# One level of Strassen's algorithm in an up-projection, and a down-projection that reads its features from DRAM

## The chip, the cores and the metric

The program runs on one core of a Trainium2 chip. The core has five engines that work side by side and meet through semaphores: TensorE (PE: matrix products into PSUM, with its weight loads shown apart as PEld), VectorE (DVE), ScalarE (ACT), GpSimd (POOL) and SyncE (SP, which here only issues DMAs). The metric is the device time of one execution in microseconds (us); a kernel's time is the median of its runs. A span is the time from the first to the last instruction of one profiled execution.

## The reference

One residual block of a streaming encoder: 1024 frames of width 1024, with 16 meta tokens in front (1040 tokens), all in float32. An input projection feeds two attention branches of 8 heads each; their outputs are projected, gated, added, and projected once more by `w_out`. Then comes the part that the change touches:

```python
h  = h + rms_norm(mixed, gains[1])                 # mixed = (gated sum) @ w_out
xn = rms_norm(h, gains[2])                         # 1040 x 1024
u  = causal_depthwise_conv(xn @ w_up, conv_w, conv_b)   # w_up 1024 x 5632, 3 taps over time
u_gate, u_val = split(u, 2)                        # 2816 each
ffn = (gelu(u_gate) * u_val) @ w_down              # w_down 2816 x 1024
h  = h + rms_norm(ffn, gains[3])
return h[:, 16:]                                   # the meta tokens are dropped
```

## The kernel before

**Layout.** Features lie on the 128 partitions, tokens along the free axis. A width of 1024 is 8 tiles of 128 (`KT`), the feed-forward width of 2816 is 22 (`NK`). From line 526 on only the last 1026 tokens are kept (`NA`: 1024 frames and the two before them, which the three taps of the convolution need), in three pieces of 342 (`PCA`).

**Products in three terms.** TensorE runs in its reduced-precision float32 mode (`F32R`). To keep the precision, each operand is split into a rounded part and a remainder (`hi`, `lo`), and `products` (line 111) adds `hi*hi + hi*lo + lo*hi`: three matmuls where one would be. A weight tile comes in through `load_w` (line 95): one DMA into `wraw` (three buffers), a cast on ACT into `whi`, a subtraction on GpSimd or VectorE into `wlo` (two buffers each).

**Stages.** Lines 61 to 523 do the attention. Lines 526 to 574 project and gate the branches. `merge(i, o)` (587) multiplies by `w_out`, piece by piece, 24 matmuls of 342 columns each; `norms(i)` (604) takes the first RMS norm of a piece, adds the residual, writes it to DRAM (`hd`), splits the sum, scaled by the second norm's gains, into `x2h` and `x2l`, and makes the second norm's factor `rs2`, by which the up-projection's result is multiplied as it leaves PSUM (line 654). So the up-projection's matmuls need the split sum, not the finished second norm. While the last piece is normalized (`tail`, lines 660 to 672), TensorE already has the first two pieces' up-projection of two weight tiles to do, ordered by hand with `after` (`tc.issue_after`).

**The feed-forward part.** `up_tile(k)` (681) makes the gate tile and the value tile of 128 features each: 3 pieces x 8 input tiles x 3 terms = 72 matmuls of 342 columns for each, then the three taps (ACT line 694, VectorE line 696 twice), the gelu (699), the product (701) and the split into `gh`, `gl`, which stay in SBUF. Groups of 4, 4, 4, 4 and 6 such tiles (`GROUPS`) are multiplied by `w_down`: `down` (714) accumulates one group in PSUM and adds it to `acc` (722, 724), one group behind the up-projection, in columns of 512. The last group goes by `last_down` (750) in columns of 256 so that the last norm (`last_norm`, 765) and the output follow each quarter.

**What sets the order.** Each engine has a queue that it works off in order. The order in it is made when the program is built: among the instructions whose inputs are due by a planner's own costs, the one that stands first in the program text goes first. Tiles of one tag share their buffers, and a pool that is opened where an earlier one was closed takes over its memory, tile by tile, each new tile waiting for the tiles that lay there (`reuse_waits="tile"`). All DMAs of this part are issued by SP, in one queue, except half of the output's, which ACT issues.

## Time and profile before

| | |
|---|---|
| median of 3 runs | 1752.41 us (1752.24 to 1753.49) |
| the profiled execution's own time | 1753.54 us |
| its span | 1751.5 us |
| mean granted TensorE clock | 0.981 |
| PE busy | 1691.4 us (97%), 10716 matmuls |
| DVE, ACT, POOL busy | 986.5, 704.3, 690.0 us |
| moved by DMA | 127.32 MB, mean 73 GB/s |

Matmuls are pipelined and their ends are modelled, so PE's busy share does not say how close it is to its peak: the rate is read from the starts of matmuls that follow one another, or from a stage's time divided by their number. A stall shows as idle time of an engine with the name of what ended it. In a group's row "x" is the number of instructions, then stand their busy time in us and the mean of one in ns.

### The profile page before, as it was taken

How to read it: one execution, taken by the hardware profiler on the slowest of the kernel's cores; microseconds unless marked ns; L12 is line 12 of the kernel's file. 1: busy time of each engine (PE TensorE's matmuls, PEld its weight loads, DVE VectorE, ACT ScalarE, POOL GpSimd, SP SyncE). 2: the span in 40 equal slices, each digit the busy share in tenths (PEclk: the TensorE clock that was granted, in tenths of full speed). 3: DMA queues.
4: the chain of work that ended last, by engine and by line, in shares of the span. 5: the costliest groups of instructions: out<-in, count | busy, mean ns of one | idle time of the engine just before them, and what ended most of it. 6: DMA issues, size and time to landing. Idle time of an engine off the chain costs nothing.

```text
span 1751.5 us, 27046 instructions
## 1 busy us (share of the span) xinstructions
PE 1691.4 (97%) x10716; PEld 1635.1 (93%) x10716; DVE 986.5 (56%) x1652; ACT 704.3 (40%) x1409; POOL 690.0 (39%) x423
## 2 busy tenths in 40 slices
...
GB/s 165 65 57 74 60 60 62 62 57 52 38 43 41 36 41 64 62 211 145 139 167 161 123 51 25 57 52 31 54 61 31 42 71 27 36 73 49 29 129 109
DMA packets 57166, 127.32 MB, mean 73 GB/s; under 512 B 10160, under 2 KB 31920, under 8 KB 56272
## 3 DMA queue, kind: packets, MB, share of 16 engines
...
## 4 chain that ended last, share of the span: by engine, by line
PE 84%; DVE 8%; issue 3%; ACT 2%; DMA 2%; POOL 1%; SPq 0%; DVEq 0%; ACTq 0%; POOLq 0%
PE pu L116 27%; PE pd L710 14%; PE pq L116 9%; PE pg L116 9%; PE y L116 5%; PE pv L116 4%; PE po L429 4%; PE pm L116 3%; PE tr L419 3%; PE s L347 2%; PE s L346 2%; DVE xl L127 1%; DVE kp L396 1%; PE tm L409 1%; DMA oraw<-od 1%
## 5 line engine op out<-in xcount | busy, mean ns | idle before, releaser
L654 DVE TENSOR_TENSOR u<-pu,rs 128x342 f32<-128x342 f32 x132 | 67.4, 513 | 260.9 <-PE pu L116 256.4
L116 PE MATMUL pu<-x2h,wl_u 128*128 128x342 f32 x1056 | 190.0, 321 | 3.7 <-DVE wl_u L90 3.7
L90 POOL TENSOR_TENSOR wl_u<-wr_u,wh_u 128x1024 fp32r<-128x1024 f32 x40 | 96.1, 2401 | 245.7 <-ACT wh_u L104 166.6
L116 PE MATMUL pu<-x2h,wh_u 128*128 128x342 f32 x1056 | 190.2, 322 | 0.6 <-DVE u L654 0.6
L116 PE MATMUL pu<-x2l,wh_u 128*128 128x342 f32 x1056 | 189.0, 321 | 0.0
L116 PEld LDWEIGHTS pu<-x2h,wl_u 128*128 128x128 f32 x1056 | 172.1, 190 | 4.0 <-DVE wl_u L90 4.0
L116 PEld LDWEIGHTS pu<-x2h,wh_u 128*128 128x128 f32 x1056 | 171.8, 190 | 1.4 <-DVE u L654 0.9
L116 PEld LDWEIGHTS pu<-x2l,wh_u 128*128 128x128 f32 x1056 | 172.1, 190 | 0.0
L696 DVE SCALAR_TENSOR_TENSOR c<-u,cb,c 128x1024 f32<-128x1024 f32 (+1 forms) x100 | 135.4, 1357 | 57.4 <-ACT c L694 55.9
L391 POOL TENSOR_SCALAR pr<-pr,mx 128x144 f32<-128x144 f32 (+3 forms) x64 | 114.9, 1801 | 102.6 <-DVE mx L390 63.6
L399 POOL TENSOR_TENSOR pr<-pr,kp 128x143 f32<-128x143 f32 (+3 forms) x64 | 80.6, 1260 | 120.9 <-DVE kp L396 69.5
L424 DVE TENSOR_TENSOR pt<-tr,pt 128x512 fp32r<-128x512 f32 (+1 forms) x160 | 98.2, 631 | 36.8 <-ACT pt L423 34.3
L429 PE MATMUL po<-pt,vv 128*128 128x256 f32 (+1 forms) x640 | 109.9, 282 | 7.7 <-DVE pt L424 5.9
L104 ACT CAST wh_u<-wr_u 128x1024 fp32r<-128x1024 f32 x44 | 46.2, 1051 | 167.1 <-PE pu L116 125.7
L429 PEld LDWEIGHTS po<-pt,vv 128*128 128x128 f32 x640 | 94.4, 190 | 9.8 <-DVE pt L424 6.9
L710 PE MATMUL pd<-gl,wh_d 128*128 128x512 f32 x256 | 101.1, 395 | 0.0
L710 PE MATMUL pd<-gh,wl_d 128*128 128x512 f32 x256 | 101.1, 395 | 0.0
L710 PE MATMUL pd<-gh,wh_d 128*128 128x512 f32 x256 | 101.1, 395 | 0.0
L423 ACT CAST pt<-tr 128x512 fp32r<-128x512 f32 (+1 forms) x160 | 83.1, 545 | 35.5 <-PE tr L419 33.8
L90 POOL TENSOR_TENSOR wl_d<-wr_d,wh_d 128x512 fp32r<-128x512 f32 x32 | 41.4, 1295 | 141.1 <-ACT wh_d L104 95.2
L419 PE MATMUL tr<-cs,pr 128*128 128x128 f32 x576 | 91.0, 274 | 0.0
L384 ACT ACTIVATE pr<-s,mx 128x144 f32<-128x144 f32 (+6 forms) x112 | 59.8, 541 | 75.9 <-DVE mx L382 60.5
...
## 6 DMA issues: line engine op xcount, KB each, us to landing
...
```

The costliest lines, as they stand in the source:

```text
L90: eng.tensor_tensor(dst, a, f(hi), op=ALU.subtract)
L116: marks["mm"] = nc.tensor.matmul(ps, w[:, k * P : (k + 1) * P], x[:, k - k0, n0:n1], start=(k == k0 and s == 0), stop=(k == k1 - 1 and s = ...
L384: nc.scalar.activation(pr[:, s0:s1], pss[k][:, : s1 - s0], AF.Exp, bias=m, scale=-1.0, accum_out=mx[:, 4 + k : 5 + k])
L391: nc.gpsimd.tensor_scalar(pr[:, :w], pr[:, :w], z, None, op0=ALU.mult)
L399: nc.gpsimd.tensor_tensor(pr[:, : w - 1], pr[:, : w - 1], kp[:, 1:w], op=ALU.mult)
L419: nc.tensor.transpose(tr[:, x * P : (x + 1) * P], prs[tb][:, NM + j * P : NM + (j + 1) * P], ident)
L423: nc.scalar.copy(pt[:, 0, :n], tr[:, :n])
L424: nc.vector.tensor_tensor(pt[:, 1, :n], tr[:, :n], f(pt[:, 0, :n]), op=ALU.subtract)
L429: nc.tensor.matmul(po[:, o0:256], vj, pt[:, s, 256 * j : min(256 * j + 256, n)], start=False, stop=(last and j == 1 and s == 1))
L654: nc.vector.tensor_tensor(u[:, n0:n1], ps, rs2[:, n0:n1], op=ALU.mult)
L696: nc.vector.scalar_tensor_tensor(cc, u[:, c0 + tap : c1 + tap], cb[:, x, tap : tap + 1], cc, op0=ALU.mult, op1=ALU.add)
L710: nc.tensor.matmul(ps, w[:, k * P : (k + 1) * P], x[:, c0:c1], start=(k == 0 and s == 0), stop=(k == len(gs) - 1 and s == 2))
```

## The change

**The up-projection** of a gate tile and its value tile is taken as one 2 x 2 block product. On the left, the weights: rows gate (`a11`, `a12`) and value (`a21`, `a22`), columns the first and second half of the 1024 input features. On the right, the normalized input: rows its two halves of features, columns two halves of tokens of 514 each (`HT`; the two tokens in the middle are in both, for the taps). In Winograd's form of Strassen's algorithm seven block products replace eight, at the price of sums: four on the weights per pair of tiles (`s1` to `s4`), four on the input once (`t1` to `t4`), and sums of the results. Each block product is 4 input tiles x 3 terms x two pieces of 258 and 256 columns (`BL`): 24 matmuls. A pair of tiles has 168 matmuls where it had 144, of 257 columns where it had 342.

**Around it.** The second norm is now applied to the input itself, before it is split (`norms`, its last loop), since the sums need a common scale. The seven right factors are split and kept in SBUF: `b11` and `b21` during the merge of the last piece, the five others after its norms, in two slices of columns (0 to 172, 172 to 514). The products that were ordered by hand under the last norms are gone, and with them `rs2`, `x2h`, `x2l`.

**The down-projection** comes after the whole up-projection. The gated features of each tile go to DRAM (`gdr`). They are read back in three column blocks of 512, 256 and 256 tokens (`DP`), split (`hidden`), and multiplied by all of `w_down` for each block (`down`), accumulating all 22 tiles in PSUM; the loads and the splits of `w_down` are done three times, in chunks of 8, 7 and 7 tiles. The additions to `acc` are gone; ACT takes the squares and the scaled copy straight from PSUM.

The core of the diff (the lines of the branch projections, lines 535 to 574, only change their indentation and the pool they are in; `parts(i)` names the token half or halves, `xh2[0]` and `xh2[1]`, into which a piece falls):

```diff
-GROUPS = [4, 4, 4, 4, 6]
+NB = NX // 2
+HT = NB + 2
+DP = [(0, 512), (512, 768), (768, 1024)]
...
+    px1 = pc.enter_context(ExitStack())
+    xc1 = px1.enter_context(tc.tile_pool(name="xc1", reuse_waits="tile", bufs=1))
+    right = {}
+    def right_tiles(pool, names):
+        for n in names:
+            right[n] = (pool.tile([P, 4, HT], F32R, name=f"rh_{n}"), pool.tile([P, 4, HT], F32R, name=f"rl_{n}"))
+    right_tiles(xc1, ("b11", "b21"))
+    pxh = ExitStack()
+    xhp = pxh.enter_context(tc.tile_pool(name="xhp", reuse_waits="tile", bufs=1))
+    xh2 = [xhp.tile([P, KT, HT], F32, name=f"xn{i}") for i in range(2)]
+    phn = ExitStack()
+    hp = phn.enter_context(tc.tile_pool(name="hp", reuse_waits="tile", bufs=1))
+    psA = pc.enter_context(tc.tile_pool(name="psA", reuse_waits="tile", bufs=4, space=PSUM))
+    psN_ = ExitStack()
+    psN = psN_.enter_context(tc.tile_pool(name="psN", reuse_waits="tile", bufs=2, space=PSUM))
...
+    def norms(i):
...
+        for k in range(KT):
+            for x, c in hs:
+                nc.scalar.activation(mg[:, k, c], x[:, k, :], AF.Copy, scale=gn[:, 2, k : k + 1])
+        rs = rstd_row(sqs, w, hp, psN, "ms", f"c{i}").unsqueeze(1)
+        for x, c in hs:
+            for k in range(0, KT, 4):
+                nc.vector.tensor_tensor(x[:, k : k + 4, :], mg[:, k : k + 4, c],
+                                        rs[:, :, c].to_broadcast([P, 4, c.stop - c.start]), op=ALU.mult)
+    def split(name, x, c, eng):
+        h, l = right[name]
+        nc.scalar.copy(h[:, :, c], x)
+        sub(eng, l[:, :, c], x, h[:, :, c])
+    for i in range(len(PCA)):
+        for o in range(KT):
+            merge(i, o)
+            if i and o == 1:
+                norms(i - 1)
+            if i == 2 and o == 4:
+                nc.gpsimd.tensor_copy(xh2[1][:, :, 0:2], xh2[0][:, :, NB : NB + 2])
+                for k, n in enumerate(("b11", "b21")):
+                    split(n, xh2[0][:, 4 * k : 4 * k + 4, :], slice(0, HT), nc.gpsimd)
+    pm.close()
+    norms(len(PCA) - 1)
+    phn.close()
+    psN_.close()
+    xc2 = pc.enter_context(tc.tile_pool(name="xc2", reuse_waits="tile", bufs=1, side="right"))
+    right_tiles(xc2, ("t2", "b22", "t3", "t4", "t1"))
+    xtp = pxh.enter_context(tc.tile_pool(name="xtp", reuse_waits="tile", bufs=1))
+    for c in (slice(0, 172), slice(172, HT)):
+        w = c.stop - c.start
+        b11, b21 = (xh2[0][:, k : k + 4, c] for k in (0, 4))
+        b12, b22 = (xh2[1][:, k : k + 4, c] for k in (0, 4))
+        t1, t2 = (xtp.tile([P, 4, WMX], F32, tag=t, name=f"{t}_{c.start}")[:, :, :w] for t in ("t1", "t2"))
+        nc.vector.tensor_tensor(t1, b12, b11, op=ALU.subtract)
+        nc.vector.tensor_tensor(t2, b22, t1, op=ALU.subtract)
+        split("t2", t2, c, nc.vector)
+        nc.gpsimd.tensor_tensor(b12, b22, b12, op=ALU.subtract)
+        split("b22", b22, c, nc.vector)
+        split("t3", b12, c, nc.gpsimd)
+        nc.vector.tensor_tensor(b21, b21, t2, op=ALU.subtract)
+        split("t4", b21, c, nc.vector)
+        split("t1", t1, c, nc.gpsimd)
+    pxh.close()
...
+    gdr = [dr.tile([P, NX], F32, name=f"gdr{k}") for k in range(NK)]
+    pu = ExitStack()
+    up = pu.enter_context(tc.tile_pool(name="up", reuse_waits="tile", bufs=2))
+    psR = pu.enter_context(tc.tile_pool(name="psR", reuse_waits="tile", bufs=2, space=PSUM))
+    BL = [(0, 258), (258, HT)]
+    def left_factors(k):
+        raws = []
+        for s in range(2):
+            raw = (wp if s == 0 else up).tile([P, KT * P], F32, tag="wraw" if s == 0 else "vraw",
+                                              bufs=3 if s == 0 else 1, name=f"wu{k}{s}")
+            nc.sync.dma_start(raw, wup[2 * k + s])
+            raws.append(raw)
+        g, v = raws
+        a11, a12, a21, a22 = g[:, 0:512], g[:, 512:1024], v[:, 0:512], v[:, 512:1024]
+        sa_ = up.tile([P, 1024], F32, tag="sA", bufs=1, name=f"sA{k}")
+        sb_ = up.tile([P, 1024], F32, tag="sB", bufs=1, name=f"sB{k}")
+        s2, s4, s3, s1 = sa_[:, 0:512], sa_[:, 512:1024], sb_[:, 0:512], sb_[:, 512:1024]
+        def two(pool, tags, bufs, n, src, eng, what):
+            h, l = (pool.tile([P, n], F32R, tag=t, bufs=bufs, name=f"{what}{t}{k}") for t in tags)
+            nc.scalar.copy(h, src)
+            sub(eng, l, src, h)
+            return h, l
+        h0, l0 = two(wp, ("whi", "wlo"), 2, 1024, g, nc.gpsimd, "a")
+        nc.gpsimd.tensor_tensor(s1, a21, a22, op=ALU.add)
+        nc.gpsimd.tensor_tensor(s2, s1, a11, op=ALU.subtract)
+        nc.gpsimd.tensor_tensor(s4, a12, s2, op=ALU.subtract)
+        h1, l1 = two(up, ("uh1", "ul1"), 1, 1024, sa_, nc.vector, "b")
+        nc.gpsimd.tensor_tensor(s3, a11, a21, op=ALU.subtract)
+        h3, l3 = two(up, ("uh3", "ul3"), 1, 512, a22, nc.gpsimd, "c")
+        h2, l2 = two(wp, ("whi", "wlo"), 2, 1024, sb_, nc.gpsimd, "d")
+        return {"a11": (h0, l0, 0), "a12": (h0, l0, 4), "s2": (h1, l1, 0), "s4": (h1, l1, 4),
+                "s3": (h2, l2, 0), "s1": (h2, l2, 4), "a22": (h3, l3, 0)}
+    turns = [0]
+    def up_pair(k):
+        lf = left_factors(k)
+        us = [up.tile([P, 2, HT], F32, tag=f"u{s}", name=f"u{k}{s}") for s in range(2)]
+        A = [psA.tile([P, 512], F32, tag="A", name=f"A{k}{j}") for j in range(2)]
+        def product(l, r, j, ps, first, last=True):
+            h, lo, k0 = lf[l]
+            xh, xl = right[r]
+            c0, c1 = BL[j]
+            for s, (w, x) in enumerate(((h, xh), (h, xl), (lo, xh))):
+                for i in range(4):
+                    nc.tensor.matmul(ps[:, : c1 - c0], w[:, (k0 + i) * P : (k0 + i + 1) * P], x[:, i, c0:c1],
+                                     start=(first and s == 0 and i == 0), stop=(s == 2 and i == 3),
+                                     skip_group_check=True)
+        def other(l, r, j):
+            turns[0] += 1
+            pool, tag = (psR, "R") if turns[0] % 2 else (pl, "lin")
+            ps = pool.tile([P, 512], F32, tag=tag, name=f"R{k}{l}{j}")
+            product(l, r, j, ps, True)
+            return ps[:, : BL[j][1] - BL[j][0]]
+        def kept(j, what):
+            w = BL[j][1] - BL[j][0]
+            t = up.tile([P, 258], F32, tag="kept", bufs=6, name=f"{what}{k}{j}")[:, :w]
+            nc.scalar.copy(t, A[j][:, :w])
+            return t
+        cols = [slice(*b) for b in BL]
+        p1, u2, u3 = [None] * 2, [None] * 2, [None] * 2
+        for j in range(2):
+            product("a11", "b11", j, A[j], True)
+            p1[j] = kept(j, "p1")
+        for j in range(2):
+            r = other("a12", "b21", j)
+            nc.vector.tensor_tensor(us[0][:, 0, cols[j]], r, p1[j], op=ALU.add)
+        for j in range(2):
+            product("s2", "t2", j, A[j], False)
+            u2[j] = kept(j, "u2")
+        for j in range(2):
+            r = other("s4", "b22", j)
+            nc.vector.tensor_tensor(us[0][:, 1, cols[j]], r, u2[j], op=ALU.add)
+        for j in range(2):
+            product("s3", "t3", j, A[j], False)
+            u3[j] = kept(j, "u3")
+        for j in range(2):
+            r = other("a22", "t4", j)
+            nc.vector.tensor_tensor(us[1][:, 0, cols[j]], r, u3[j], op=ALU.add)
+        for j in range(2):
+            product("s1", "t1", j, A[j], False)
+            d = us[1][:, 1, cols[j]]
+            nc.scalar.copy(d, A[j][:, : BL[j][1] - BL[j][0]])
+            nc.gpsimd.tensor_tensor(u3[j], d, u3[j], op=ALU.subtract)
+            e = us[0][:, 1, cols[j]]
+            nc.gpsimd.tensor_tensor(e, e, u3[j], op=ALU.add)
+        return us
+    def conv_gate(k, us):
+        cv = []
+        for s in (1, 0):
+            x, u = 2 * k + s, us[s]
+            c = up.tile([P, 2, NB], F32, tag=f"c{s}", bufs=1 if s else 2, name=f"c{x}")
+            cv.append(c)
+            nc.scalar.activation(c, u[:, :, 2 : 2 + NB], AF.Identity, bias=cb[:, x, 3:4], scale=cb[:, x, 2:3])
+            for tap in (1, 0):
+                nc.vector.scalar_tensor_tensor(c, u[:, :, tap : tap + NB], cb[:, x, tap : tap + 1], c,
+                                               op0=ALU.mult, op1=ALU.add)
+        v, g = cv
+        nc.scalar.activation(g, g, AF.Gelu_apprx_tanh)
+        nc.vector.tensor_tensor(g, g, v, op=ALU.mult)
+        nc.sync.dma_start(gdr[k], g.rearrange("p h t -> p (h t)"))
+    for k in range(NK):
+        conv_gate(k, up_pair(k))
+    pu.close()
+    px1.close()
...
+        dp = pd.enter_context(tc.tile_pool(name="dp", reuse_waits="tile", bufs=2))
+        psD = pd.enter_context(tc.tile_pool(name="psD", reuse_waits="tile", bufs=4, space=PSUM))
+        psM = pd.enter_context(tc.tile_pool(name="psM", reuse_waits="tile", bufs=2, space=PSUM))
+        CK = [(0, 8), (8, 15), (15, NK)]
+        def hidden(t):
+            c0, c1 = DP[t]
+            r = []
+            for k in range(NK):
+                raw = dp.tile([P, 512], F32, tag="graw", bufs=4, name=f"gr{t}{k}")[:, : c1 - c0]
+                nc.sync.dma_start(raw, gdr[k][:, c0:c1])
+                h = dp.tile([P, 512], F32R, tag="gh", bufs=30, name=f"gh{t}{k}")[:, : c1 - c0]
+                l = dp.tile([P, 512], F32R, tag="gl", bufs=30, name=f"gl{t}{k}")[:, : c1 - c0]
+                nc.scalar.copy(h, raw)
+                sub(turn(k), l, raw, h)
+                r.append((h, l))
+            return r
+        def down(t, gs):
+            c0, c1 = DP[t]
+            w = c1 - c0
+            acc = dp.tile([P, KT, 512], F32, tag="acc", name=f"acc{t}")[:, :, :w]
+            sas = dp.tile([P, 512], F32, tag="sas", name=f"sas{t}")[:, :w]
+            for o in range(KT):
+                ps = psD.tile([P, 512], F32, tag="dn", name=f"pd{t}{o}")[:, :w]
+                for j, (k0, k1) in enumerate(CK):
+                    hi, lo = load_w(wdn[o][:, k0 * P : k1 * P], (k1 - k0) * P, f"d{t}{o}{j}", turn(o + j))
+                    for k in range(k0, k1):
+                        gh, gl = gs[k]
+                        for s, (a, x) in enumerate(((hi, gh), (hi, gl), (lo, gh))):
+                            nc.tensor.matmul(ps, a[:, (k - k0) * P : (k - k0 + 1) * P], x,
+                                             start=(k == 0 and s == 0), stop=(k == NK - 1 and s == 2))
                 if o == 0:
+                    nc.scalar.activation(sas, ps, AF.Square)
                 else:
+                    s2 = dp.tile([P, 512], F32, tag="fs", name=f"fs{t}{o}")[:, :w]
+                    nc.scalar.activation(s2, ps, AF.Square)
+                    nc.vector.tensor_tensor(sas, sas, s2, op=ALU.add)
+                nc.scalar.activation(acc[:, o, :], ps, AF.Copy, scale=gn[:, 3, o : o + 1])
...
+        todo = None
+        for t in range(len(DP)):
+            res = down(t, hidden(t))
+            if todo:
+                last_norm(*todo)
+            todo = (t, *res)
+        last_norm(*todo)
```

356 lines of the change are left out of this document (119 added, 237 removed).

## The prediction

> **What bounds the kernel now.** I read the page's busy shares and chain of waits, then cut the execution into stages and counted matmuls in each, then followed single instructions where the change cuts in.
>
> ```profile
> span 1751.5 us, 27046 instructions
> PE 1691.4 (97%) x10716; PEld 1635.1 (93%) x10716; DVE 986.5 (56%) x1652; ACT 704.3 (40%) x1409; POOL 690.0 (39%) x423
> PE 84%; DVE 8%; issue 3%; ACT 2%; DMA 2%; POOL 1%; SPq 0%; DVEq 0%; ACTq 0%; POOLq 0%
> ```
>
> TensorE sets the end: 84% of the chain is its own work. The sum is made against the profiled execution's 1753.54 us (span 1751.5), 1.1 above the median.
>
> By stage (window, length, then busy time and count of PE, PEld, DVE, ACT, POOL, granted clock, DMA share, GB/s): the merge, the change to the up-projection, up- and down-projection, the last group, the tail. Below, the same for the up-projection's tile `pu` (two windows) and the down-projection's `pd` (PE, PEld, DVE first).
>
> ```profile
> 865.40:969.90 104.50, 100.02 (x614) 98.24 (x614) 67.13 (x61) 54.99 (x92) 40.93 (x14) 0.97 0.53 177
> 969.90:1017.00 47.10, 41.18 (x235) 39.28 (x233) 34.80 (x47) 16.88 (x24) 1.67 (x1) 0.89 0.23 78
> 1017.00:1666.60 649.60, 649.60 (x3744) 614.57 (x3745) 250.26 (x288) 172.49 (x184) 192.49 (x95) 1.00 0.16 47
> 1666.60:1738.00 71.40, 70.68 (x590) 70.33 (x589) 46.90 (x99) 36.00 (x77) 11.76 (x8) 1.00 0.40 118
> 1738.00:1751.50 13.50, 2.78 (x15) 1.79 (x13) 6.10 (x11) 1.48 (x4) 2.49 (x2) 0.61 0.27 91
> ```
> ```profile
> 969.90:1017.00 47.10, 35.44 (x192) 33.03 (x191) 3.97 (x8) 0.89 0.23 78
> 1017.00:1666.60 649.60, 471.06 (x2976) 470.57 (x2976) 62.97 (x123) 1.00 0.16 47
> 1017.00:1666.60 649.60, 179.82 (x768) 144.16 (x769) 33.16 (x48) 9.30 (x16) 1.00 0.16 47
> ```
>
> From 1017.0 to 1666.6 TensorE never stops, at clock 1.00: 2976 matmuls of 342 columns at 0.1583 us and 768 of 512 at 0.2341. POOL is busy 30% of that stretch, DVE 39%. The price of 256 columns is read from the last group's starts (25 rows, 24 steps in 2.85 us):
>
> ```profile
> 1735.83 0.28 PE L710 MATMUL pd<-gh,wll 128*128 128x256 f32 x1
> ...
> 1738.68 0.29 PE L710 MATMUL pd<-gh,wll 128*128 128x256 f32 x1
> ```
>
> 0.1188 us each, and by interpolation 0.1197 for 258.
>
> **Step 1, TensorE's own work.** Up before: 44 x 72 = 3168 x 0.1583 = 501.5 us. After: 22 x 168 = 3696, half of 258 and half of 256: 1848 x (0.1197 + 0.1188) = 440.8. **-60.7**; one pair takes 20.03. The down-projection goes from 768 x 0.2341 + 576 x 0.1188 = 248.2 to 528 x 0.2341 + 1056 x 0.1188 = 249.1: **+0.9**.
>
> **Step 2, the pace of a pair.** Strassen's sums go to GpSimd and VectorE, so how these two share SBUF matters:
>
> ```profile
> 1044.05 2.40 POOL L90 TENSOR_TENSOR wl_u<-wr_u,wh_u 128x1024 fp32r<-128x1024 f32 x1 [1.44 <-PE pu L116]
> 1045.69 3.16 DVE L696 SCALAR_TENSOR_TENSOR c<-u,cb,c 128x1024 f32<-128x1024 f32 x2 [1.32 <-ACT c L694]
> 1091.22 2.61 DVE L696 SCALAR_TENSOR_TENSOR c<-u,cb,c 128x1024 f32<-128x1024 f32 x2 [1.32 <-ACT c L694]
> 1242.70 1.30 POOL L90 TENSOR_TENSOR wl_d<-wr_d,wh_d 128x512 fp32r<-128x512 f32 x1 [4.71 <-ACT wh_d L104]
> 1242.74 0.68 DVE L724 TENSOR_TENSOR acc<-pd,acc 128x512 f32<-128x512 f32 x1
> 912.75 3.59 DVE L618 TENSOR_TENSOR xr<-mixed,xr 128x1368 f32<-128x1368 f32 x1
> 914.86 4.49 POOL L618 TENSOR_TENSOR xr<-mixed,xr 128x1368 f32<-128x1368 f32 x1
> ```
>
> Two taps take 2.61 us alone (1091.22). At 1045.69 they take 3.16: GpSimd's subtraction ends at 1046.45, and the taps end 2.40 after that, as if they had begun only then. At 914.86 it is the other way: VectorE ends at 916.34, GpSimd 3.01 later. An addition with an operand in PSUM (1242.74, 0.68) passes beside GpSimd unhindered. So a GpSimd operation and a VectorE operation with both inputs in SBUF exclude each other, and their times add. The Trainium skill says the same ("SBUF — State Buffer", section "SBUF: two separate sides"): the two engines share a port pair that the first to start holds for its whole instruction. By that rule alone, with no operation shortened, a pair takes at least the plain sum below, and this step costs 39 us instead of the 28.7 that I take.
>
> The prices:
>
> ```profile
> L90 POOL TENSOR_TENSOR wl_u<-wr_u,wh_u 128x1024 fp32r<-128x1024 f32 x40 | 96.1, 2401 | 245.7 <-ACT wh_u L104 166.6 <-PE pu L116 79.1
> L90 POOL TENSOR_TENSOR wl_d<-wr_d,wh_d 128x512 fp32r<-128x512 f32 x32 | 41.4, 1295 | 141.1 <-ACT wh_d L104 95.2 <-PE pu L116 45.8
> L654 DVE TENSOR_TENSOR u<-pu,rs 128x342 f32<-128x342 f32 x132 | 67.4, 513 | 260.9 <-PE pu L116 256.4 <-ACT rs L635 4.4
> L104 ACT CAST wh_u<-wr_u 128x1024 fp32r<-128x1024 f32 x44 | 46.2, 1051 | 167.1 <-PE pu L116 125.7 <-PE pd L710 32.6 <-issue 8.8
> 1196.32 1.22 DVE L701 TENSOR_TENSOR c<-c,c 128x1024 f32<-128x1024 f32 x1
> ```
>
> GpSimd costs 0.189 us + 2.16 ns a column (from 512 and 1024). A pair issues there two of 1024, five of 512 (`s1` to `s4`, the remainder of `a22`), four of about 257: 4.80 + 6.48 + 2.98 = 14.26 us. VectorE has with both inputs in SBUF four taps at 1.30, one remainder and one product at 1.22: 7.64. Sum 21.9 us a pair against TensorE's 20.03. Its six additions out of PSUM (each under 0.513) are free of this. The upper bound has no end at 21.9: both queues are in order, and a wait in one holds the port's next user; I allow 24. The lower bound shortens both engines by what the blocked rows show (2.40 for 2.61, 3.01 for an estimated 3.14): about 20.7; below that stands 20.03, the cover being complete. I take 21.4, since GpSimd has work of the next pair to fill its waits: 1.37 x 21 pairs = **+28.7** (0 to +83).
>
> **Step 3, from merge to up-projection.** Here TensorE loses its cover.
>
> ```profile
> 968.48 1.53 PE L116 MATMUL pm<-mh,wl_wo 128*128 128x342 f32 x8 [0.89 <-POOL wl_wo L90]
> 979.66 1.41 PE L136 MATMUL rp_b<-cs,sa 128*128 128x1 f32 x6 [0.73 <-DVE sa L602]
> 986.89 0.87 DVE L617 TENSOR_TENSOR mixed<-mixed,rr_b 128x684 f32<-128x684 f32 x1 [4.72 <-PE rr_b L149]
> 909.76 3.07 DVE L617 TENSOR_TENSOR mixed<-mixed,rr_b 128x1368 f32<-128x1368 f32 x2 [0.17 <-PE rr_b L149]
> 993.28 1.67 POOL L618 TENSOR_TENSOR xr<-mixed,xr 128x684 f32<-128x684 f32 x1 [24.86 <-ACT x2h L126]
> 995.94 1.34 ACT L628 ACTIVATE sq<-xr 128x1368 f32<-128x1368 f32 x1
> 1000.25 2.69 DVE L632 TENSOR_REDUCE ss<-sq 128x342 f32<-128x1368 f32 x1
> 1008.48 0.59 PE L146 MATMUL rr_c<-dg_c,one_sq 128*128 128x256 f32 x2
> ```
>
> Before, the last merge ends at 970.0 and the last norm's factor is there at 1009, 39 us later; meanwhile TensorE did 192 up matmuls, 30.4 of the window's 47.1 us. The lost 16.7 go: **-16.7**. After, only pair 0's first two products (48 matmuls, 5.7 us) need no more than `b11` and `b21`. The third waits for three things in a row. First the last `norms`: 39 as measured, about 25 by its operations alone (the waits at 979.66 and 1000.25 fall away with the old splits); but the remainders of `b11` and `b21`, two GpSimd operations of 2056 columns (4.6 us each), now hold the port there: 32. Second the five split factors, which cannot begin earlier: their scratch tiles lie where piece 2's `mixed` lay. VectorE has six operations of 688 (0.87) and six of 1368 (1.54), 14.5 us; GpSimd three of 1.67 and three of 3.14, 14.4; on one port 28.9. Third pair 0's value weights: `vraw` lies over `xh2[0]`, free when `t4` is split (26 of the 28.9); then a 512 KB load (3.0 at the merge's 177 GB/s; behind it on SP wait the next pairs' loads), `s1`, `s2`, `s4` (3.9) and a cast (1.05): 8. Restart at 32 + 26 + 8 = 66 us after the merge (45 if the port is shared well and the norms take 25; 80 if they take 39 and SP is late).
>
> ```profile
> 932.10 0.59 PE L136 MATMUL rp_c<-cs,ss 128*128 128x1 f32 x2 [2.17 <-DVE ss L632]
> 934.69 2.48 PE L116 MATMUL pm<-mh,wl_wo 128*128 128x342 f32 x8
> 944.09 1.42 PE L116 MATMUL pm<-ml,wh_wo 128*128 128x342 f32 x8
> ```
>
> After an idle spell the matmuls run at about half speed for a while (2.48 us for eight against 1.42): +2. Idle in all 66 + 2 - 5.7 = **+62.3** (41 to 76). In the merge itself the 16 scaled remainders of the first two norms leave VectorE, on which TensorE waits at 932.10: **-3** (-6 to +3).
>
> **Step 4, from up to down.** `gl` and the later `gh` buffers lie over the up-projection's `u`, `c` and right factors, so 22 tiles are split only after the last product: GpSimd 11 x 1.295, VectorE 11 x 0.69 (estimated from 0.87 and 1.54), 21.8 us on one port, beside the last tile's own taps and product (6.4) and the weights of the first output tile (some 2). TensorE needs 66 x 0.2341 = 15.5 for that output tile. About 30 against 15.5: **+15** (5 to 25). The last tile's trip through DRAM hides under it.
>
> **Step 5, the down-projection's weights.** `w_down` is loaded and split three times. At 512 columns a chunk of 8 tiles lasts 24 x 0.2341 = 5.6 us, ample. At 256 it lasts 2.85 (2.49 for 7), but with two buffers the next-but-one chunk needs a cast (1.05) and a remainder (GpSimd 2.40, VectorE 1.22) within its neighbour's time: 3.45 on GpSimd. By chunk about 0.8, 0.4 and 0 us late in turn, some 4.5 us for each of the two blocks, and 3 for the port: **+12** (0 to 24). Cover gone for SP too: 72 loads, 66 read-backs and their waits stand in its one queue. ACT's 92 us of casts over 250 have room, and the tail keeps its 256 columns: 0.
>
> Sum: -60.7 + 0.9 + 28.7 - 16.7 + 62.3 - 3 + 15 + 12 = +38.5; 1753.5 + 38.5 = 1792, as a median **1791 us**.
>
> **Rivals.** *The port does not bind* (the other side): GpSimd and VectorE overlap in these shapes. Then the pair goes at 20.03 (-28.7), the restart comes at 47 (-19), step 4 costs 6 (-9), step 5 less by 3: 1731, faster. It decides from about two thirds of that overlap on (38.5 of 59.7). For it: both engines have slack in a pair's 20 us, 14.3 and 10; against: the rows at 1045.69 and 914.86. *The queues pile up*: ACT, waiting in order for GpSimd's late sums, holds the copies out of PSUM, and TensorE waits too: 24 us a pair, +55: 1846. For: the sums of pair k end in the same queue that makes pair k+1's factors; against: factors are due a whole pair later. *The change-over is short*: the first slice (172 columns, pieces 0 and 1 only) is split under the merge and the weights come early: restart at 35, 1760. Against: the shared memory named above. *Seven products save nothing*: 128 x 128 weight loads bound a matmul at 0.158 whatever its width, +144 in the up-projection: 1935. Against: 0.1188 at 256 columns.
>
> **Chances.** Forecast 0.53, port 0.16, pile-up 0.15, short change-over 0.14, no saving 0.02. The range, 1742 to 1842, leaves out most of the port case (0.12) and half of the pile-up with what is above it (0.09). Within 0.2% (3.5 us, what this kernel's runs can tell apart) 0.05, lying between the port and the change-over case; faster 0.16; slower 0.79.
>
> **What would show it.** TensorE idle some 60 us between the last `pm` and the first `s2` product, ended by GpSimd or VectorE; the up stage at 21.4 us a pair with short PE waits, GpSimd over 65% busy and lengthened taps; 15 us lost at the first `pd`; chunk waits on `wl_d` in the 256-column blocks. The prediction is wrong if the pair runs at 20.0, or the gap after the merge is under 40.

## The result, and the profile after

The changed kernel takes 1857.69 us (median of 4 runs, 1855.81 to 1858.73) against 1752.91 (4 runs, 1752.24 to 1753.49): 1.0597 times as long, 95% interval 1.0578 to 1.0615. It is slower by 105 us; forecast were 38 (1791, range 1742 to 1842). The sign was right, the size was not, and the range did not hold the time.

The page's busy row of the changed kernel, then the shares of its chain of waits:

```profile
PE 1670.7 (90%) x11482; PEld 1611.8 (87%) x11482; DVE 1114.0 (60%) x1618; ACT 830.4 (45%) x1678; POOL 1004.6 (54%) x646
PE 51%; DVE 14%; POOL 12%; ACT 8%; issue 8%; DMA 5%; SPq 1%; ACTq 0%; DVEq 0%; POOLq 0%
```

TensorE's own work is 51% of the chain where it was 84%. VectorE, GpSimd, ACT and DMA together have 39% of it; they had 13%. The matmuls' saving is in the trace; the time went into places where TensorE waits, and the stages show which. The columns are window, length, busy time and count of PE, PEld, DVE, ACT and POOL, granted clock, DMA share and GB/s; the rows are the merge, the gap to the first `s2` product, the rest of the up-projection, the change to the down-projection, its 512-column block up to the copy of its last output out of PSUM, then the first 256-column block with the first output of the second, the other seven outputs of the second, and the tail.

```profile
863.90:985.30 121.40, 108.66 (x629) 106.74 (x628) 70.06 (x58) 57.28 (x103) 42.16 (x17) 0.89 0.56 158
985.30:1064.90 79.60, 22.58 (x102) 20.26 (x100) 53.91 (x34) 25.93 (x32) 43.35 (x18) 0.57 0.11 31
1064.90:1528.20 463.30, 440.85 (x3624) 436.60 (x3624) 281.04 (x257) 204.15 (x322) 353.65 (x233) 0.99 0.21 73
1528.20:1544.00 15.80, 0.05 (x2) 0.01 (x1) 7.80 (x6) 4.98 (x7) 3.49 (x3) 0.62 0.39 123
1544.00:1688.50 144.50, 133.49 (x554) 105.87 (x554) 48.06 (x41) 53.15 (x85) 52.49 (x35) 0.95 0.45 133
1688.50:1784.60 96.10, 80.63 (x595) 76.67 (x596) 43.63 (x46) 40.15 (x68) 42.16 (x26) 0.91 0.66 201
1784.60:1845.20 60.60, 56.87 (x454) 54.63 (x452) 20.04 (x18) 22.87 (x33) 25.21 (x12) 1.00 0.58 168
1845.20:1856.80 11.60, 1.25 (x6) 0.82 (x6) 5.57 (x10) 1.01 (x3) 2.49 (x2) 0.68 0.68 226
```

From these rows, the prediction's terms and what was measured (us against before):

| part | predicted | measured | how it is worked out |
|---|---|---|---|
| ahead of the merge | 0 | -1.5 | the merge starts at 863.9 for 865.4 |
| merge | -3 | +16.9 | 121.4 - 104.5 |
| step 3, gap after the merge | +62.3 | +73.9 | 79.6 - 5.7 of products that run in it |
| before's loss there | -16.7 | -16.7 | 47.1 - 30.4, gone |
| steps 1 and 2, up-projection | -32.0 | -32.5 | 463.3 + 5.7 - 501.5 |
| step 4, up to down | +15 | +30.9 | 15.8 + 138.7 - 123.6 of 528 matmuls at 0.2341 |
| step 5, narrow blocks | +12 | +37.1 | 162.5 - 125.4 of 1056 at 0.1188 |
| step 1, down-projection's matmuls | +0.9 | +0.9 | taken as its base in the two rows above |
| tail | 0 | -1.9 | 11.6 - 13.5 |
| sum | +38.5 | +107.1 | the profiled executions differ by 105.0 |

In the rows for steps 4 and 5 the boundary is the first matmul of 256 columns, at 1682.65; 26 of these run ahead of 1688.5, where the window above ends. The sum misses the measured difference by 2 us: before's last group took 71.4 us where its 576 matmuls at 0.1188 count 68.4, and its up-projection stage 649.6 where its matmuls count 650.9; the table enters neither. Four terms were too small, by 20 (merge), 12 (gap), 16 (step 4) and 25 us (step 5). The sections below take them one by one, and the up-projection with them, whose number fits.

**How single times are read.** Where no number of runs is given, a kernel was run once. The stages that an edit does not touch vary between kernels: where the code is the same, the merge takes 119 to 121 us and the down-projection 297 to 301 from its first matmul to its last, and the changed kernel is the longest in both; the gap takes 79.5 to 80.0. So an edit is judged by the length of its own stage; the whole time stands beside it.

### The profile page after: what moved, and what is told of

Its sections match the earlier page's. It is cut to its first block, busy times and chain, and to the rows that moved or that the text cites. A ratio compares the mean times of both kernels' runs of the same rounds, so it can differ in the third digit from the quotient of the medians.

```text
span 1856.8 us, 29591 instructions
## 1 busy us (share of the span) xinstructions
PE 1670.7 (90%) x11482; PEld 1611.8 (87%) x11482; DVE 1114.0 (60%) x1618; ACT 830.4 (45%) x1678; POOL 1004.6 (54%) x646
## 4 chain that ended last, share of the span: by engine, by line
PE 51%; DVE 14%; POOL 12%; ACT 8%; issue 8%; DMA 5%; SPq 1%; ACTq 0%; DVEq 0%; POOLq 0%
PE pd L852 9%; PE pg L118 8%; PE pq L118 8%; DVE c L807 6%; PE y L118 5%; PE pv L118 4%; PE po L431 4%; PE pm L118 3%; PE tr L421 3%; POOL sB L730 2%; POOL u L794 2%; POOL dwlo L92 2%; POOL wl_d L92 2%; PE s L349 2%; PE s L348 2%
## 5 line engine op out<-in xcount | busy, mean ns | idle before, releaser
L807 DVE SCALAR_TENSOR_TENSOR c<-u,cb,c 128x1024 f32<-128x1024 f32 x88 | 191.8, 2180 | 146.0 <-ACT c L805 145.1
L852 PE MATMUL pd<-gh,wh_d 128*128 128x256 f32 (+1 forms) x528 | 173.7, 329 | 17.4 <-ACT gh L835 16.1
L852 PE MATMUL pd<-gh,wl_d 128*128 128x256 f32 (+1 forms) x528 | 174.9, 332 | 15.8 <-POOL wl_d L92 13.5
L852 PE MATMUL pd<-gl,wh_d 128*128 128x256 f32 (+1 forms) x528 | 172.6, 327 | 5.0 <-POOL gl L92 3.3
L92 POOL TENSOR_TENSOR wl_d<-wr_d,wh_d 128x896 fp32r<-128x896 f32 (+1 forms) x36 | 79.8, 2217 | 148.2 <-ACT wh_d L106 140.8
L852 PEld LDWEIGHTS pd<-gh,wl_d 128*128 128x128 f32 x528 | 103.4, 196 | 28.5 <-POOL wl_d L92 18.8
L852 PEld LDWEIGHTS pd<-gh,wh_d 128*128 128x128 f32 x528 | 103.8, 197 | 27.9 <-ACT gh L835 17.9
L852 PEld LDWEIGHTS pd<-gl,wh_d 128*128 128x128 f32 x528 | 103.6, 196 | 15.4 <-POOL gl L92 6.0
L398 DVE TENSOR_TENSOR_SCAN kp<-kp 128x16 f32<-128x16 f32 (+3 forms) x64 | 89.1, 1394 | 0.4
L348 PE MATMUL s<-k,q 128*128 128x264 f32 (+9 forms) x240 | 80.1, 338 | 0.0
L753 PE MATMUL A<-rh_t,dwhi 128*128 128x256 f32 (+1 forms) x352 | 58.6, 289 | 22.4 <-ACT u L767 22.4
```

The lines of the kernel that those rows point to most:

```text
L92: eng.tensor_tensor(dst, a, f(hi), op=ALU.subtract)
L348: nc.tensor.matmul(ps[:tn, :n], q2[:, t0 : t0 + tn], k1[:, s0:s1], start=True, stop=False)
L398: nc.vector.tensor_tensor_scan(r, r, r, kp[:, w - P : w - P + 1], op0=ALU.mult, op1=ALU.bypass)
L807: nc.vector.scalar_tensor_tensor(c, u[:, :, tap : tap + NB], cb[:, x, tap : tap + 1], c, op0=ALU.mult, op1=ALU.add)
L852: nc.tensor.matmul(ps, a[:, (k - k0) * P : (k - k0 + 1) * P], x, start=(k == 0 and s == 0), stop=(k == NK - 1 and s == 2))
```

## The experiments

### The pace of a pair: is it the port?

Step 2 was predicted at 21.4 us a pair from the sum of what GpSimd and VectorE need of SBUF, and measured at (463.3 - 14.3 of pair 0's last products) / 21 = 21.4. But the chain around one such pair, in the timeline of the changed kernel (start, length, engine, line), has another shape:

```profile
1304.78 2.40 POOL L92 TENSOR_TENSOR awlo<-wu,awhi 128x1024 fp32r<-128x1024 f32 x1
1304.88 3.37 DVE L807 SCALAR_TENSOR_TENSOR c<-u,cb,c 128x1024 f32<-128x1024 f32 x1 [3.73 <-ACT c L805]
...
1308.51 1.97 DVE L807 SCALAR_TENSOR_TENSOR c<-u,cb,c 128x1024 f32<-128x1024 f32 x1
1310.52 1.06 ACT L810 ACTIVATE c<-c 128x1024 f32<-128x1024 f32 x1 [5.42 <-DVE c L807]
...
1312.42 0.64 ACT L767 COPY u<-A 128x258 f32<-128x258 f32 x2
1312.84 0.75 PE L753 MATMUL A<-rh_t,dwhi 128*128 128x258 f32 x4 [1.02 <-ACT u L767]
```

The last two taps take 3.37 and 1.97 us beside GpSimd for 1.30 alone. The gelu stands next in ACT's queue and waits 5.42 us for them. Behind it in the same queue stands the copy of `A` out of PSUM, for which TensorE waits. The rows permit two theories: the port is full (A), or the port only makes the taps late, and the order of ACT's queue carries that to TensorE (B). e1 leaves every operation as it is and moves the gelu of pair k, with the product and the store that follow it, in the queues to behind the `u3` copies of pair k+1:

```diff
             u3[j] = kept(j, "u3")
+        if k:
+            gate_store(k - 1)
...
-        v, g = cv
-        nc.scalar.activation(g, g, AF.Gelu_apprx_tanh)
+        gates[k] = cv
+    def gate_store(k):
+        v, g = gates.pop(k)
+        with after(marks["kept"] if k < NK - 1 else None):
+            nc.scalar.activation(g, g, AF.Gelu_apprx_tanh)
```

> The changed kernel with one thing moved: in ScalarE's queue the GELU of a pair stands behind the next pair's two u3 copies out of PSUM instead of ahead of them; the work is the same. Changed kernel: 1857.7 us, 21.3 us a pair. Theory A, the prediction's step 2 (the shared port is full: GpSimd 16.3 us and VectorE 10.6 us of every 21.3): the wait only moves, the pair stays at 21.0 to 21.4, time 1851 to 1860. Theory B (the port only makes the taps late; TensorE loses its 1.2 us a pair because the copy out of PSUM stands in order behind a GELU that waits for those taps): the pair goes to 20.1 to 20.4, TensorE's wait on the copies falls from some 22 us to under 5, time 1832 to 1840.

1836.07 us, 22 less. The up-projection's row of e1:

```profile
1064.20:1509.60 445.40, 439.15 (x3624) 434.85 (x3624) 302.02 (x257) 204.25 (x322) 362.83 (x233) 1.00 0.22 76
```

And from its list of waits (total, times, longest), the copies out of PSUM, 22.4, 20 and 3.1 in the changed kernel:

```profile
PE A L754 <- ACT u L768: 6.2, 20, 1.1
```

The stage loses 17.9 us; a pair takes (445.4 - 14.3) / 21 = 20.5, half a microsecond above TensorE's 20.03, and the waits for these copies fall by 16.2. Pace and waits lie just outside what theory B set for itself (20.1 to 20.4, under 5) and below theory A's 21.0 to 21.4. So theory B holds in the main: the queue's order cost 18 of the 28 us, and the sum of 21.9 us of port time is no floor. The Trainium skill ("SBUF — State Buffer", section "SBUF: two separate sides") says that two such operations shut each other out for the whole instruction. The lengthened taps agree with it; that the profile's durations can be added up as lock times does not follow from it, and here that sum is 1.4 us a pair too long. My estimate is that the fixed part of each operation (0.19 us on GpSimd by the prediction's line through its two sizes) does not hold the port: the first tap above ends 1.07 us after GpSimd's operation, and takes 1.30 alone. No run measures that by itself. With the shortened times of the prediction's lower bound the sum is 20.7, close to the 20.5; whether the port still sets the half microsecond that is left is open.

### The merge: what comes before the matmuls

From the changed kernel's timeline of the merge (start, length, engine, line, and in brackets the idle time before it and what ended it): DMAs of SyncE's queue (SPq), a cast that waited for weights, and the same eight matmuls after an idle spell and later.

```profile
866.41 8.93 SPq L633 DMA_DIRECT2D xn<-in_xb  x4
875.45 3.09 SPq L99 DMA_DIRECT2D wr_wo<-in_wout  x3
...
925.83 0.58 SPq L644 DMA_DIRECT2D hd<-xn  x1
...
940.63 1.04 ACT L106 CAST wh_wo<-wr_wo 128x1024 fp32r<-128x1024 f32 x1 [8.55 <-DMA wr_wo<-in_wout]
...
942.52 2.65 PE L118 MATMUL pm<-mh,wh_wo 128*128 128x342 f32 x8 [3.57 <-ACT s L623]
...
963.77 1.42 PE L118 MATMUL pm<-mh,wh_wo 128*128 128x342 f32 x8
```

The loads of the residual into `xn` go out in one run of 8.93 us, with the next weights behind them in SP's one queue. Behind them TensorE waits 5.1 us once for a cast of weights (at 888.2). Later the store of `hd`, which waits for the norm, goes out at 925.83 (in before at 919.37, in the same place), ahead of the next weights (929.61), and the cast at 940.63 waits 8.55 us for these to land. The copies of finished products stand behind that cast in ACT's queue, and TensorE waits for them at 942.52. e2 gives the loads of a piece out later, behind the weight load of the sixth tile of the merge:

```diff
-        for x, c in hs:
-            nc.sync.dma_start(x, xb[:, :, n0 + c.start : n0 + c.stop])
...
             merge(i, o)
+            if o == 5:
+                x_load2(i)
```

> The changed kernel, with the loads of the residual input queued one piece at a time behind the weight load of the sixth merge tile of that piece, instead of all four together at 866 us. Merge stage of the changed kernel 121.4 us against 104.5 before. Theory A (4 MB of loads at once make the next merge weights late: TensorE waited 5.1 us for a cast at about 885 and ran cold behind it): merge stage 111 to 115, time 1847 to 1852. Theory B (the merge is longer because the norms' chain is longer): 119 to 123, time 1855 to 1860.

1848.00 us, 10 less. The merge's row:

```profile
866.90:978.30 111.40, 102.90 (x629) 100.84 (x627) 71.72 (x61) 57.79 (x103) 42.57 (x17) 0.95 0.64 172
```

111.4 us for 121.4, and for the 119 to 121 of the other kernels with the loads in their old place: the loads' place was worth 7 to 10 of the 17, as theory A had it. The rest stayed; its waits are 3.35 us for the same copies and 3.90 for a norm's factor on VectorE (the `hd` store's place and the norms were not tried alone). Each stall is paid twice: after the idle 3.57 us eight matmuls took 2.65 us for 1.42. The Trainium skill ("TensorE: Matmul & The Clock Gate", Part 1) has the array fall to half its clock after an idle window of about 3.4 us; these two rows agree, 1.9 times as long behind 3.57 us. The slow clock outlasts the stall by far: in the changed kernel's merge the granted clock was 0.50 for 27 us (in one piece from 941.4 to 961.9), in before's for 7, while TensorE's idle time grew from 4.5 to 12.7 us. So about half of the 17 us is idle time, and by my estimate from these numbers the clock has most of the other half.

### The gap after the merge

In the changed kernel's timeline the gap has the three parts of step 3: the norms, the five factors, pair 0's value weights. These rows mark them (the first two show the remainder of `b11`/`b21` on GpSimd beside the norm's operation on VectorE):

```profile
988.75 9.40 POOL L92 TENSOR_TENSOR rl_b<-xn,rh_b 128x2056 fp32r<-128x2056 f32 x2 [0.97 <-ACT rh_b L667]
988.98 4.70 DVE L624 TENSOR_TENSOR sa<-sa,s 128x342 f32<-128x342 f32 x1
...
1022.73 0.88 DVE L691 TENSOR_TENSOR t<-xn,xn 128x688 f32<-128x688 f32 x1
...
1049.53 14.63 SPq L715 DMA_DIRECT2D wu<-in_wup  x3
...
1057.86 2.39 POOL L92 TENSOR_TENSOR dwlo<-sB,dwhi 128x1024 fp32r<-128x1024 f32 x1
1060.19 2.37 POOL L92 TENSOR_TENSOR awlo<-wu,awhi 128x1024 fp32r<-128x1024 f32 x1
1062.50 1.31 POOL L732 TENSOR_TENSOR sA<-wu,sA 128x512 f32<-128x512 f32 x1
...
1064.94 1.23 PE L753 MATMUL A<-rh_t,buh 128*128 128x258 f32 x4 [1.11 <-ACT buh L725]
```

The norms end at 1022.7 (37 after the merge; 32 predicted): an addition of 342 columns, at 988.98, is held up for 4.70 us by GpSimd's 9.40. The factors take to 1049.5 (26.7; 26 predicted). The last part takes 15.4 for 8: the load needed 3.4 (3.0 predicted), but GpSimd's queue had two remainders (1057.86, 1060.19) that nobody yet waited for ahead of `s4` (1062.50). e3 makes the factors' sums and remainders on VectorE alone:

```diff
-                    split(n, xh2[0][:, 4 * k : 4 * k + 4, :], slice(0, HT), nc.gpsimd)
+                    split(n, xh2[0][:, 4 * k : 4 * k + 4, :], slice(0, HT), nc.vector)
...
-        nc.gpsimd.tensor_tensor(b12, b22, b12, op=ALU.subtract)
+        nc.vector.tensor_tensor(b12, b22, b12, op=ALU.subtract)
...
-        split("t3", b12, c, nc.gpsimd)
+        split("t3", b12, c, nc.vector)
```

(and `t1` as `t3`)

> The changed kernel with the seven right factors' work all on VectorE: the remainders of b11, b21, t3 and t1 and the difference b22 - b12 leave GpSimd. Between merge and up-projection the changed kernel took 79.6 us, of it 26.7 for the five last factors. Theory A (the two engines exclude each other on one port, so that GpSimd's 2.16 ns a column only cost more than VectorE's 1.02): the five factors take 20 to 23, the norms ahead of them 2 to 4 less, 79.6 becomes 69 to 74, time 1847 to 1853. Theory B (they overlap, the work is shared): the factors take 27 to 34 on one engine, time 1858 to 1866.

1844.30 us, 13 less. The gap:

```profile
983.60:1054.50 70.90, 22.78 (x103) 20.95 (x101) 45.68 (x42) 26.16 (x32) 14.25 (x10) 0.60 0.13 35
```

70.9 for 79.6, in the range of theory A (the whole time is 3 us below it), and the factors about 20 for 26.7. Here two engines that shut each other out were no faster than one; the work was cheaper on the one with the shorter operations (1.23 us for a remainder of 1024 columns on VectorE, 2.40 on GpSimd).

### The down-projection

Three experiments on the 317 us from the last up product to the last down product. They start from these rows of the changed kernel's timeline (the last gated tile's store, the read-backs in SP's queue and the first matmul behind them; then the two matmul groups of block 1's norm) and from one line of TensorE's waits.

```profile
1538.48 0.33 SPq L812 DMA_DIRECT2D gdr<-c  x1
1538.90 19.93 SPq L832 DMA_DIRECT2D gr<-gdr  x15
1543.99 0.80 PE L852 MATMUL pd<-gh,wh_d 128*128 128x512 f32 x1 [15.75 <-ACT gh L835]
...
1765.09 0.98 PE L138 MATMUL rp_d<-cs,sas 128*128 128x1 f32 x4 [4.97 <-DVE sas L859]
...
1768.76 1.19 PE L148 MATMUL rr_d<-dg_d,one_sq 128*128 128x256 f32 x2 [2.69 <-DVE dg_d L144]
```
```profile
PE pd L852 <- POOL wl_d L92: 13.5, 16, 3.6
```

Every read-back stands behind the store of the last tile in one queue, and that store behind the last tile's taps, gelu and product. So TensorE stands for 15.8 us; nothing runs ahead under which the trip through DRAM could hide. Until the first output tile is copied out of PSUM 37.4 us pass, at the rate at which tiles come in (27 matmuls of the second output run in them too); the seven others follow by 15.3 in the mean. Counted by matmuls, the wide block takes 138.7 us and the two narrow ones 162.5. In the narrow blocks the chunks wait for GpSimd's `wl_d`: block 1 takes 77.5 us where its matmuls need 62.7. Its norm stands in TensorE's queue ahead of block 2's first product: 4.97 and 2.69 us of idling, 10.3 us from block 1's last matmul to block 2's first, and then matmuls at about half speed (0.21 us for 0.119, at a granted clock of 0.50). Block 2 takes 74.8 us from there.

e4 has two blocks of 512 columns instead of 512, 256, 256:

```diff
-DP = [(0, 512), (512, 768), (768, 1024)]
+DP = [(0, 512), (512, 1024)]
```

> The changed kernel with the down-projection in two blocks of 512 columns instead of 512, 256 and 256: the weights are loaded and split twice, not three times. From the trace of the changed kernel the two narrow blocks lose 9 us (first) and 22 us (second, 16 of them in its first output, where TensorE waits for the norm of the block before and for weights, then runs at half speed). Theory A (narrow blocks with two weight buffers are the loss): these 31 us go, the second wide block loses some 6 in its first output to the read-back and the tail is some 7 longer: time 1836 to 1846. Theory B (the loss is the change from block to block, whatever the width, and the longer tail takes the rest): 1854 to 1864.

1819.07 us, 39 less, the most of any single edit. The down-projection from its first matmul, and the tail:

```profile
1541.30:1798.30 257.00, 248.90 (x1066) 201.33 (x1066) 83.95 (x66) 87.75 (x122) 87.37 (x47) 0.98 0.45 136
1798.30:1817.30 19.00, 2.12 (x10) 1.26 (x10) 9.83 (x9) 1.43 (x3) 4.65 (x2) 0.64 0.72 259
```

257.0 for 301.2, with 7.4 more in the tail; that is more than either theory allowed (1836 at the least). By matmuls, the first block takes 133.5 us, which is within the 133 to 139 of the kernels that leave it as it is, and the rest 123.4 for 162.5, where 528 wide matmuls need 123.6 and 1056 narrow ones 125.4. So the whole loss of the narrow blocks, 37 us, is gone: the second block of 512 columns hardly waits for weights (`wl_d` 3.0 us in all for 13.5), only one block's norm stands among another's products, and a third of the weight loads and splits are gone. How much each of these is worth was not taken apart.

e5 keeps the three blocks and makes every remainder of the down-projection on VectorE:

```diff
-                sub(turn(k), l, raw, h)
+                sub(nc.vector, l, raw, h)
...
-                    hi, lo = load_w(wdn[o][:, k0 * P : k1 * P], (k1 - k0) * P, f"d{t}{o}{j}", turn(o + j))
+                    hi, lo = load_w(wdn[o][:, k0 * P : k1 * P], (k1 - k0) * P, f"d{t}{o}{j}", nc.vector)
```

> The changed kernel with every remainder of the down-projection (read-back tiles and weights) on VectorE, none on GpSimd. Changed kernel 1857.7 us; its first output tile took 37 us for 15.5 us of matmuls, and in the narrow blocks TensorE waited 13.5 us for weight remainders of GpSimd (2.1 to 2.4 us each, on VectorE 1.1 to 1.2). Theory A (one port: GpSimd's slower passes only add up): first output 28 to 32, the waits for GpSimd gone and under 4 us of them left for VectorE: time 1836 to 1845. Theory B (the read-back through SP and DRAM sets the first output, ScalarE's casts the narrow blocks): under 5 us gained, 1852 to 1858.

1836.81 us, 21 less; 278.5 for 301.2 from the first matmul to the last:

```profile
1544.40:1822.90 278.50, 260.00 (x1600) 231.26 (x1600) 132.12 (x172) 116.16 (x184) 7.62 (x4) 0.97 0.59 175
```

The blocks lost 52 us against their matmuls (301.2 - 249.0); 19 to 23 of these came from having half of the remainders on GpSimd (the other kernels' 297 to 301 make the range), 13 to 17 of them in the narrow blocks. In this kernel the first output took 33 us for 37.4, and from the fifth to the last read-back of the first block they followed each other by 1.28 us for 1.42. From the fifth on each waits in the queue until a remainder has freed its raw buffer, except a few that follow another directly. So the loop of four raw buffers and one queue set that pace, not the 21.8 us of port time in step 4, which is 1.0 a tile. Buffers and queue were not tried apart.

e6 asks whether the store ahead of the read-backs is what holds TensorE for 15.8 us. The last gated tile is made in a weight buffer, and its store is issued behind the first four read-backs:

```diff
-        nc.sync.dma_start(gdr[k], g.rearrange("p h t -> p (h t)"))
+        if k < NK - 1:
+            nc.sync.dma_start(gdr[k], g.rearrange("p h t -> p (h t)"))
...
+                if t == 0 and k == 3:
+                    nc.sync.dma_start(gdr[NK - 1], held[0].rearrange("p h t -> p (h t)"))
```

> The changed kernel with the store of the last gated tile queued on SP behind the first four read-backs of the down-projection instead of ahead of them (that tile lies in a weight buffer meanwhile). In the changed kernel TensorE stood 15.8 us between the last product at 1528.2 and the first down matmul; SP issued the first read-back at 1538.9, right behind that store at 1538.5, which waits for the last tile's taps and GELU. Theory A (SP's order makes the read-back late): the first read-back is issued by 1531, the gap falls to 6 to 11, time 1849 to 1854. Theory B (port, ScalarE and memory of the last pair hold the split up anyway): gap 13 to 16, time 1855 to 1859.

1862.56 us: no gain, and the idle time 17.0 for 15.8. SP's queue in the timeline, and a wait in it from the list of waits:

```profile
1524.87 17.75 SPq L99 DMA_DIRECT2D wr_d<-in_wdn  x4
1542.71 1.81 SPq L838 DMA_DIRECT2D gr<-gdr  x4
```
```profile
SPq L99 <- DVE wl_d L92: 11.0, 1, 11.0
```

The read-backs no longer stand behind the store, they stand behind a load of `w_down` that waits 11.0 us for its buffer. The one wait was replaced by the next in the same queue, and the edit has a part in it: the held tile takes one of the three weight buffers. Both theories were missed (13 to 16 us idle at the most). Whether the store alone would have held the read-backs stays open by this run; e10 answers it for the queue as a whole.

### Does the form itself pay?

e7 leaves Strassen's sums out. The seven products become eight plain ones on the same halves, with the same two token pieces; only `b12` and `b22` are split after the merge, `s1` to `s4` and `t1` to `t4` are gone, and so each half of the result is the plain sum of two products:

```diff
-    right_tiles(xc2, ("t2", "b22", "t3", "t4", "t1"))
+    right_tiles(xc2, ("b12", "b22"))
...
+                    product(f"a{s + 1}1", f"b1{h + 1}", j, ps, True, False)
+                    product(f"a{s + 1}2", f"b2{h + 1}", j, ps, False, True)
```

> The changed kernel with the eight plain block products in place of Strassen's seven: the sums of the left and right factors, the copies and additions of the results and three right factors are left out, the rest (norms, halves, conv, trip through DRAM, down-projection in one accumulation) stays. 192 matmuls a pair at 0.1192 = 22.9 us against the 21.3 measured with seven: +35 in the up-projection. Against it the change-over: two late factors to split instead of five (26.7 to about 10) and no sums ahead of the first casts (15.4 to about 8): -24. Theory A (Strassen's gain is spent at the change-over): time 1860 to 1876, the gap between merge and up-projection 52 to 60. Theory B (the gap comes from norms and loads that stay): gap 72 to 80, time 1882 to 1895.

1853.49 us. From the last merge matmul to the last up product:

```profile
987.20:1528.50 541.30, 516.98 (x4254) 515.35 (x4253) 257.63 (x239) 169.25 (x218) 69.39 (x28) 0.97 0.20 68
```

541.3 for the changed kernel's 79.6 + 463.3 = 542.9. The eighth product costs 22 x 24 = 528 more matmuls, 62.9 us, and the kernel without the sums is as fast (both theories had it slower, at 1860 or more): as the change was built, the sums cost all that the form saves.

### Mending the waits

e8 takes the edits of e1 to e4 together.

> The changed kernel with four edits together: GELU behind the next pair's copies (alone -22 us), residual loads one piece at a time (-10), right factors on VectorE (-13), down-projection in two blocks of 512 (-39). If the four losses lie in stages of their own, they add: 1857.7 - 84 = 1774, 1769 to 1779. If a later stage takes back what an earlier one gains (a shared limit), 1785 to 1805.

1789.12 us. Gap 69.0, up-projection 444.6, idle 15.3, down-projection 258.3, tail 20.2: with the merge's 115.0 the stages that the four edits touch keep nearly all their gains (70 us together, 73 in the single runs). By the time alone the other theory, a later stage that takes gains back (1785 to 1805), would have been right; the stages do not show it. The single runs' whole times add to 84 us; what they had beyond 73 was the variation of stages that no edit touches.

e9 starts from e8 and attacks the gap. Pair 0's value weights, their sums and the factor of `s2` and `s4` get memory of their own and are made early, on VectorE; `b11` and `b21` are split after the first row of the last norm, in halves:

```diff
+    with after(marks["rt_b2"]), after(marks["dg_b2"]):
+        for k, n in enumerate(("b11", "b21")):
+            for c in (slice(0, 258), slice(258, HT)):
+                split(n, xh2[0][:, 4 * k : 4 * k + 4, c], c, nc.vector)
...
+    raws0, sa0 = raw_factors(0)
...
+    b0 = two(0, up0, ("uh1", "ul1"), 1, 1024, sa0, nc.vector, "b")
```

> The kernel with the four edits (1789.1 us) and, in the gap between merge and up-projection, three more: pair 0's value weights, sums and second factor lie in memory of their own and are made ahead of the right factors, on VectorE; the b11 and b21 factors stand in the queues behind the last norm's first row, in halves. In the four-edit kernel this gap takes 69.0 us: 33 of norms, 20 of factors, 15 of loading pair 0's value weights, its sums on GpSimd behind other work, and a cast. Theory A (a chain in a row: what is taken out of it is gained): the 15 go, TensorE starts as soon as t2 is split, gap 44 to 54, time 1764 to 1775. Theory B (the port or the weight loads: the sums only delay the norms and the factors): gap 62 to 70, time 1782 to 1791.

1777.53 us; the gap 54.5 for 69.0, of which the rest of the up-projection gives 4 back, and, from the list of waits, one that was not there before:

```profile
979.10:1033.60 54.50, 20.44 (x99) 18.51 (x99) 46.40 (x45) 24.13 (x32) 3.60 (x3) 0.66 0.11 26
```
```profile
PE A L774 <- ACT p L788: 14.4, 1, 14.4
```

The copy of pair 0's first product (at 1033.13) goes into memory where tiles of the norms and factors lay, and it stands in ACT's queue right behind a cast that waited for the last factor's remainder on VectorE, which ends at 1032.57. So the `s2` products wait until all factors are split. Which of the two held the copy, its memory or the queue, is not shown.

e10 starts from e8 and attacks the down-projection: remainders on VectorE, eight raw buffers for four (and 28 split tiles for 30), and the read-backs in GpSimd's DMA queue, past SP's:

```diff
-                raw = dp.tile([P, 512], F32, tag="graw", bufs=4, name=f"gr{t}{k}")[:, : c1 - c0]
-                nc.sync.dma_start(raw, gdr[k][:, c0:c1])
+                raw = dp.tile([P, 512], F32, tag="graw", bufs=8, name=f"gr{t}{k}")[:, : c1 - c0]
+                nc.gpsimd.dma_start(raw, gdr[k][:, c0:c1])
...
-                sub(turn(k), l, raw, h)
+                sub(nc.vector, l, raw, h)
```

> The kernel with the four edits (1789.1 us) and, in the down-projection: all remainders on VectorE, eight raw buffers for the read-back instead of four, and the read-backs in GpSimd's DMA queue instead of SP's. In the four-edit kernel TensorE stood 15.2 us before the first down matmul and took some 32 us for the first output of 15.0; SP issued the read-backs 1.26 us apart. Theory A (the loop of four buffers and SP's order set the pace of the read-back): idle 8 to 12, first output 20 to 25, time 1769 to 1779. Theory B (the last pair's taps, GELU and casts in the in-order queues of VectorE and ScalarE set it): idle 13 to 16, first output 27 to 33, time 1782 to 1790.

1774.11 us; the change-over and the down-projection:

```profile
1495.20:1504.60 9.40, 0.00 (x0) 0.00 (x0) 7.05 (x6) 4.76 (x7) 7.79 (x11) 0.71 0.60 174
1504.60:1752.10 247.50, 245.03 (x1066) 200.38 (x1066) 99.77 (x112) 86.40 (x121) 24.76 (x38) 0.99 0.47 143
```

15.3 fell to 9.4 and 258.3 to 247.5, as theory A had it. With the read-backs out of SP's queue some 6 us of step 4's wait are gone. The 9.4 that stay are not the last tile's trip through DRAM: its store goes out at 1505.38, when the first product has begun. They are ACT's queue once more. The first read-back has landed at 1502.46, but its cast stands behind the last gelu, which waited for VectorE's taps:

```profile
1503.03 1.06 ACT L822 ACTIVATE c<-c 128x1024 f32<-128x1024 f32 x1 [2.67 <-DVE c L815]
1503.99 2.16 ACT L848 CAST gh<-gr 128x512 fp32r<-128x512 f32 x4
```

e11 joins e9 and e10.

> The four edits (1789.1 us), the edits in the gap after the merge and those of the read-back together. By stages that add: 1745 to 1760 us. With 1753 for the kernel before, the ratio then lies between 0.995 and 1.004: Strassen's seven products then just pay for what stands around them. If the gap stays at 62 to 70: 1765 to 1775.

1765.59 us (5 runs, 1762.68 to 1767.53) against 1755.34: 1.0054 times before's, interval 1.0036 to 1.0071. The gap stayed at 54.4, the wait for the copy at 14.6. The gains of e9 and e10 (12 and 15 us) add to within 3 us; the 1745 to 1760 that were expected had counted on more from each.

e12 gives pair 0 a way past that copy: its first two products are summed in PSUM, `s1` and `s3` get memory of their own, in the down-projection `acc` lies where nothing late lay, and the last norm's residual has two more buffers.

```diff
-            product(l, r, j, ps, True)
+            if k == 0 and l == "a12":
+                product("a11", "b11", j, ps, True)
+            product(l, r, j, ps, k > 0 or l != "a12")
```

> The kernel with all edits so far (1765.6 us, 1.0054 of the kernel before) and three more, each on a wait that its trace shows: pair 0 sums its first two products in PSUM and its s1 and s3 lie in memory of their own (TensorE waited 14.6 us for a copy whose target lay over the norms' tiles); the down-projection's accumulator lies over the last convolution tiles, so that the first split tiles do not (VectorE and ScalarE waited 5 us for the last store); two more buffers for the residual in the last norm (1.8 us). Theory A (a chain in a row): 6 to 9, 4 to 6 and 1 to 3 us go: 1748 to 1756, ratio 0.995 to 1.000. Theory B (the next wait in line takes their place): 1760 to 1766, ratio 1.003 to 1.006.

1762.04 us (6 runs, 1756.79 to 1768.16) against 1753.63: 1.0052, interval 1.0033 to 1.0071. That is theory B's 1760 to 1766: the next wait took the place of the old. Pair 0's products no longer wait for the copy, but the gap is 59.4 us. The row that holds it, the end of VectorE's run beside it, and the matmul behind it:

```profile
1014.74 16.88 POOL L92 TENSOR_TENSOR awlo<-wu,awhi 128x1024 fp32r<-128x1024 f32 x1 [8.15 <-ACT awhi L704]
1026.34 3.07 DVE L92 TENSOR_TENSOR rl_t<-xn,rh_t 128x1368 fp32r<-128x1368 f32 x2
1029.52 0.76 DVE L805 COPY u<-R0a 128x258 f32<-128x258 f32 x2
1031.67 2.08 PE L775 MATMUL A<-rh_b,awlo 128*128 128x258 f32 x8 [12.57 <-POOL awlo L92]
```

A subtraction that takes 2.40 us elsewhere took 16.88 on GpSimd, through an unbroken run of VectorE operations with two SBUF inputs. That run ends at 1029.41, and the subtraction 2.21 us later, as if it had only begun then. e13 moves this one subtraction to VectorE:

```diff
-        h0, l0 = two(k, wp, ("whi", "wlo"), 2, 1024, g, nc.gpsimd, "a")
+        h0, l0 = two(k, wp, ("whi", "wlo"), 2, 1024, g, nc.vector if k == 1 else nc.gpsimd, "a")
```

> The last kernel (1762.0 us, ratio 1.0052) with one instruction moved: the remainder of pair 1's first factor on VectorE instead of GpSimd. In its trace that GpSimd subtraction took 16.88 us instead of 2.35, while VectorE ran its own two-input operations without a break, and TensorE, in order, stood 12.6 us behind it. Theory A (it never got the port, and pair 0's next product needs nothing of it): the first s2 product starts 6 to 9 us earlier after the last merge matmul (59.4 becomes 50 to 53), time 1752 to 1757, ratio 0.998 to 1.002. Theory B (TensorE then waits for the factors t2 to t4 instead): 57 to 60, time 1760 to 1764.

1762.38 us (6 runs, 1756.56 to 1763.57) against 1753.95: 1.0044, interval 1.0027 to 1.0060. `s2` starts 48.3 us after the merge, sooner than theory A had it, and the up-projection ends no sooner: 504.1 us after the merge for e12's 503.5, and the time is theory B's. From its list of waits:

```profile
PE A L775 <- DVE bul L92: 5.5, 1, 5.5
```

The 12.6 us wait is gone, and the next ones in line (5.5 for `bul`, and two of about 3) have its place.

e14 is e13 with eight plain products, without Strassen's sums and without pair 0's early weights and sums (e9), as e7.

> The same kernel with eight plain products a pair in place of Strassen's seven (no factor sums, two late right factors instead of five, no additions of products), all edits at the other stages kept. Theory A (with the waits around them removed, the seven products pay): up-projection 22 x 22.9 = 504 us and a gap some 12 us shorter than with seven: 30 to 45 us slower than the kernel with seven, 1785 to 1800. Theory B (what Strassen saves on TensorE it still loses at the change-over, as with 1853.5 against 1857.7 before the edits): within 8 us of it, 1748 to 1764.

1784.83 us, 22.5 more than e13. From the last merge matmul to the last up product:

```profile
976.50:1508.60 532.10, 514.73 (x4249) 513.48 (x4249) 248.41 (x245) 167.96 (x221) 57.60 (x31) 0.98 0.21 71
```

532.1 for 504.1. So with the waits mended the form is worth 28 us in its stage, of the 62.9 that its matmuls save. In whole time theory A had expected 30 to 45 us, theory B at most 8. In e14 TensorE has no wait in the up-projection once the norms are done. Of the 28, e14 gets some back at the change to the down-projection, whose first matmul comes after 2.4 us of idling for e13's 9.5 (its second after 3.5 more), and 22 are left in the time.

No kernel here is faster than before; e12 and e13, which their runs do not tell apart, come closest, at 1.0052 and 1.0044 times its time. What keeps e13 there: the gap and the up-projection take 504 us with 441 of matmul, so 63 are lost where before lost 17; 9.5 us idle ahead of the down-projection; a tail of 19.8 us behind the last product for 12.5; and a merge of 113.0 us for 104.6 (e11 and e12: 110.4 and 108.3).

## Why the prediction was right, and where it failed

**The sign, and the rivals.** Right. *The port does not bind* is ruled out by the lengthened taps; its pair of 20.03 us was nearly reached in e1, by another order, with the port as busy as before. *The queues pile up* was right in its mechanism in more places than its own: it was priced at 24 us a pair in the up-projection, and there came to 21.4. *The change-over is short* fell, at 79.6 us. *Seven products save nothing* fell as far as matmuls go: they run at the rate predicted (step 1 below).

**Step 1, TensorE's work.** Right as far as the price goes: in the up-projection's starts 258 columns follow each other by 0.120 us and 256 by 0.118 to 0.119 in the median (0.1197 and 0.1188 predicted).

**Step 2, the pace of a pair.** The number was right (21.4), by luck as much as by its reason. The step that failed is the use of "their times add" as the pace: 18 of its 28 us came from the gelu, which waited at the head of ACT's queue with the copies out of PSUM behind it (e1). The pile-up rival had that mechanism ("ACT, waiting in order for GpSimd's late sums, holds the copies out of PSUM"), with another late operation: VectorE's taps. The whole-instruction rule that the prediction put beside it, 39 us by its sum, was no bound either.

**The merge.** Failed, by 20 us: -3 predicted, +16.9 measured. The step looked at what left VectorE and did not count the moved DMAs: the residual's four loads stand ahead of weights in SP's queue (7 to 10 us by e2; the rest was not taken apart, and the store of `hd` stands ahead of weights in before too), and after each stall comes the slow clock (0.50 for 27 us of the stage, 7 before).

**Step 3, the gap.** Mechanism right, size 11.6 short. Its three parts in a row were as told. The terms that were mis-sized are the norms (37 for 32) and the value weights (15.4 for 8): the prediction counted `s1`, `s2`, `s4` and the cast, not what stands between them in GpSimd's queue.

**Step 4, up to down.** Failed, by 16 us. "The last tile's trip through DRAM hides under it" is the sentence that is wrong: every read-back stood behind the last tile's store, so it lay ahead of the splitting, not under it (15.8 us of idling; 9.4 in e10, where the read-backs no longer stand there and the last gelu in ACT's queue is what is left). And 22 splits were priced by the port at 21.8 us, 1.0 a tile, where the loop of four raw buffers and one queue makes 1.42 (1.28 in e5).

**Step 5, the narrow blocks.** Failed, by 25 us. The chunk waits are there, on `wl_d`, as told, but the step took them for a start-up cost of 4.5 us a block; they recur at nearly every output (block 1 takes 77.5 us for 62.7). The norm of block 1 ahead of block 2's products, with its clock loss, is not in the prediction at all: 10.3 us between the two blocks, and 13.0 us for the first 66 matmuls behind it, which need 7.8. e4, which has no narrow block, lost nothing there: 123.4 us for 123.6.

**The range.** Three of the four terms lay outside their own bounds (merge -6 to +3, step 4 5 to 25, step 5 0 to 24; measured 17, 31 and 37). The bounds were made from the operations' durations, and all the misses go the same way. What was missed each time is the order of one queue and what stands at its head, and the slow clock behind each stall.
